# Gathered rows on VectorE in half rows, one behind every 1.6th weight half

## The chip, the cores and the metric

The kernel runs on one core of a Trainium2 chip. The metric is device time in microseconds (us) of one execution. Below, PE is TensorE, DVE is VectorE, ACT is ScalarE, POOL is GpSimd and SP is SyncE, as in the profile; L119 is line 119 of the kernel.

## What is computed

One layer of a decoder trunk over 256 tokens of width 2048 in float32: an RMS norm with two parallel head groups, a cross-attention over 256 memory tokens, and PEER, a retrieval among 16384 experts of one neuron each. The change is in PEER, and only there:

```
q = (xt @ w_pq).reshape(T, PEER_HEADS, 2, PK_DIM // 2)
...
# 8 heads pick 16 experts each for every token: ids, gate
u = u_tab[idb]
act = gelu(einsum('td,thkd->thk', xb, u))
coef = gb * act
out = einsum('thk,thkd->td', coef, v_tab[idb])
...
return rmsnorm(x + out, g_final)
```

## The kernel before

All products run on PE in split precision: a float32 weight is cut into a high part (`whi`, a cast on ACT, L118) and a low part (`wlo`, a subtraction on DVE, L119), and PE multiplies with both. `wsplit` does this for a weight tile of 128 x 2048 in two halves of 1024 columns; three buffers of each kind hold halves (`bufs=3`), and three hold whole weight tiles as they come from memory (`wst`, 1 MB each, loaded by SP's queue, L105).

PEER is computed in two ways at once. For 192 of the tokens all 16384 experts are computed densely: `u_block` (L639 on) takes one tile of 128 experts, makes their activations (32 matmuls, L643 and L644, then an addition on DVE at L647 and Gelu on ACT at L648) and stores them in a ring, and `v_tile` multiplies a tile of `v` with the coefficients of its group (20 matmuls, L873 to L876; behind the last of four tiles DVE adds two results to the residual, L880). The experts come in eight groups e of 16 blocks; a group has 16 v tiles. `coef_half` (L850, and L169 and L170 by `split_plain`) turns the activations of a group into coefficients, with gates that were written to DRAM and are loaded as `gl` by SP's queue. In group e the u tiles of group e+2 are computed beside: two before each half of the coefficients, the other twelve one behind each of the first twelve v tiles, the last four v tiles having none. The groups e=6 and e=7 have no u tiles.

For the other 64 tokens the experts that were picked are gathered: 64 rows of `u_tab` and 64 of `v_tab`, each 128 x 2048 (a row for each partition), by an indirect DMA of POOL (L911) into three buffers (tag `row`). DVE takes a u row with the token's own input and accumulates the products to one number (L924, into `sact`), and adds a v row times its coefficient to `srow` (L927). The generator `gathered` holds this work; it fetches two rows ahead, and each `next` lets one row pass. It is called behind a whole `v_tile`, as often as to have passed 128 rows after 104 v tiles (`slots`, L950), so one or two rows stand behind a v tile. No rows follow the u tiles.

The order of instructions on each engine is made by a scheduler that goes by the order in which they are written and by when it takes their inputs to be ready. `keep_in_program_order` ties an instruction behind the one written just before it for the same engine; what is written later is not tied by it. Each engine runs its own instructions in that order, and one that waits holds up those behind it.

At the end (e=7) `folded` adds `srow` to the last result on PE, `finish` takes squares and the final gains (`gfin`, loaded into a buffer of tag `row`), and the result is normalised and written.

Of the kernel before, what the change touches and what calls it, by code (L numbers as in the profile page):

```python
# [10 lines left out]
F32 = mybir.dt.float32  # L11
# [42 lines left out]
def hybrid_layer(ctx: ExitStack, tc: tile.TileContext, a, out):  # L54
# [40 lines left out]


    n_w = [0]

    def wbuf():
        n_w[0] += 1  # L100
# [10 lines left out]
    def wsplit(st, order=(0, 1)):  # L111

        parts = {}
        for i in order:
            hi = wp.tile([P, 1024], F32R, tag="whi", name=f"whi{n_w[0]}_{i}", bufs=3)
            lo = wp.tile([P, 1024], F32R, tag="wlo", name=f"wlo{n_w[0]}_{i}", bufs=3)
            src = st[:, i * 1024:(i + 1) * 1024]
            S.copy(hi, src)  # L118
            V.tensor_tensor(lo, src, hi.bitcast(F32), op=OP.subtract)  # L119
            parts[i] = hi, lo  # L120

        def part(which):
            return lambda at, n=P: parts[at // 1024][which][:, at % 1024:at % 1024 + n]
        return part(0), part(1)
# [47 lines left out]
    def spread_stats(part, name):  # L172
        ps = sm_tile()
        PE.matmul(ps[:, :T], ones, part, start=True, stop=True)
        r = cst.tile([P, T], F32, name=f"rstd_{name}")
        rstd_of(r, ps[:, :T], D)
        return r

# [450 lines left out]
    with tc.tile_pool(name="ph3", bufs=2) as p3:  # L629
# [2 lines left out]
        srow = p3.tile([P, D], F32, name="srow", bufs=1)  # L632
        sids = p3.tile([P, NP], U32, name="sids", bufs=1)
        sgate = p3.tile([P, NP], F32, name="sgate", bufs=1)
        sact = p3.tile([P, NP], F32, name="sact", bufs=1)
        hpm = lambda k: hp[:, k, :]
        hs = p3.tile([P, KC, 2 * TD], F32R, name="hsc", bufs=1)

# [200 lines left out]
        with tc.tile_pool(name="ph3v", bufs=2) as pv:  # L839
# [65 lines left out]
            def gathered():  # L905

                def fetch(n):
                    if n >= 2 * NP:
                        return None
                    row = pv.tile([P, D], F32, tag="row", name=f"row{n}", bufs=ROWS)  # L910
                    nc.gpsimd.indirect_dma_start(  # L911
                        row, None, a["v_rows" if n >= NP else "u_rows"],
                        bass.IndirectOffsetOnAxis(ap=sids[:, n % NP:n % NP + 1], axis=0))
                    return row

                rows = [fetch(n) for n in range(ROWS - 1)]
                for n in range(2 * NP):
                    rows.append(fetch(n + ROWS - 1))
                    row, j = rows.pop(0), n % NP
                    if n == NP:  # L920
                        S.activation(sact, sact, AF.Gelu)
                        V.tensor_tensor(sact, sact, sgate, op=OP.mult)
                    if n < NP:
                        tc.keep_in_program_order(V.scalar_tensor_tensor(  # L924
                            row, row, 1.0, xrow, op0=OP.mult, op1=OP.mult, accum_out=sact[:, j:j + 1]))
                    else:
                        tc.keep_in_program_order(V.scalar_tensor_tensor(  # L927
                            srow, row, sact[:, j:j + 1], srow, op0=OP.mult, op1=OP.add))
                    yield

            gather = gathered()
            n_gat, n_slot, slots = 0, 0, (NE - 1) * 16 - 8
            gfin = None
            for e in range(NE):
                us = list(range((e + 2) * EB, min((e + 3) * EB, NB)))
# [6 lines left out]
                    if half < 2:  # L942
                        coef_half(e, half)
                for dq, bg in vs:
                    if n_slot == slots + 2:
                        gfin = pv.tile([P, D], F32, tag="row", name="gfin", bufs=ROWS)
                        nc.sync.dma_start(gfin, a["gfin"])
                    v_tile(e, dq, bg, e + 2 >= NE)
                    n_slot += 1
                    while n_gat < min(2 * NP, 2 * NP * n_slot // slots):  # L950
                        next(gather)
                        n_gat += 1
                    if us:
                        u_block(us.pop(0))

# [105 lines left out]
```

## Time and profile before

| | |
|---|---|
| time, median of 3 runs | 2366.49 us (2365.39 to 2367.17) |
| the profiled execution | 2376.57 us |
| its span, first to last instruction | 2374.8 us |
| PE busy | 2209.7 us, 93% of the span |
| DVE busy | 1843.8 us, 78% |
| ACT busy | 1176.4 us, 50% |
| granted TensorE clock, mean | 0.977 |
| DMA, mean over the span | 250 GB/s |

The profile is of one execution. The page gives busy times by engine, the span in slices, and the costliest groups of instructions; further views give busy time by windows, who waited for whom, and the instructions in order of time. Matmuls are pipelined and their ends are modelled, so the busy time of PE is not a measure of its peak. The stage that the change touches begins at about 1195 us.

### The profile page before, as it was taken

What the parts mean: (1) busy time and instruction counts of PE and PEld (TensorE: products, weight loads), DVE (VectorE), ACT (ScalarE), POOL (GpSimd) and SP (SyncE); (2) the same over time, 40 slices, a digit from 0 to 9 for tenths busy, and PEclk for the clock granted to TensorE, in tenths of its full rate; (3) what the DMA queues carried; (4) which work ended last, traced back from release to release, by engine and by line L of the source; (5) the groups of instructions that cost most, each with busy time, mean ns of one, the idle gap of its engine ahead of it and who ended that gap; (6) DMA issues with size and microseconds to landing.
All of it is one profiled execution on the core that took longest, in us unless ns stands there. A gap on an engine that the chain in (4) does not pass through costs nothing.

```text
span 2374.8 us, 31447 instructions
## 1 busy us (share of the span) xinstructions
PE 2209.7 (93%) x12000; PEld 1930.1 (81%) x12000; DVE 1843.8 (78%) x2754; ACT 1176.4 (50%) x1703; POOL 235.3 (10%) x132
## 2 busy tenths in 40 slices
PE   8999999999999988789979999899899899998897
PEld 6888888888888867789968888788788788887675
DVE  7887868744555698999957888878887978888864
ACT  6555547444444543557644444444444445444353
POOL 0000000000000000000001212212221222124100
PEclk9999999999999999999989999999999999999998
DMA  7444445545454533356779899999888998998963
GB/s 268 160 160 160 142 152 203 179 169 179 166 177 165 190 135 132 124 177 249 250 278 350 321 350 349 347 332 375 330 332 320 338 371 338 336 364 331 360 214 124
DMA packets 107928, 593.58 MB, mean 250 GB/s; under 512 B 9600, under 2 KB 35200, under 8 KB 38528
## 3 DMA queue, kind: packets, MB, share of 16 engines
q1 hardware_dynamic: 87472, 444.69, 51.8%
q0 software_dynamic: 18432, 134.23, 15.2%
q10 hardware_dynamic: 1872, 12.65, 1.3%
q8 instruction: 94, 1.54, 0.3%
q14 instruction: 58, 0.48, 0.1%
HBM read 576.84 MB, written 14.68 MB: 249 GB/s over the span
## 4 chain that ended last, share of the span: by engine, by line
PE 64%; issue 15%; DVE 12%; DMA 4%; POOL 3%; ACT 1%; DVEq 0%; POOLq 0%; ACTq 0%
PE mm L133 16%; PE mm L643 9%; PE mm L134 8%; PE mm L644 5%; DVE wlo L119 4%; PE sm L874 4%; PE sm L873 4%; POOL row L911 3%; PE mm L146 2%; PE mm L147 2%; DMA row<-in_v_rows,sids 2%; PE mm L145 2%; PE sm L876 2%; PE sm L808 2%; DVE row L924 1%
## 5 line engine op out<-in xcount | busy, mean ns | idle before, releaser
L119 DVE TENSOR_TENSOR wlo<-wst,whi 128x1024 fp32r<-128x1024 f32 x800 | 969.6, 1222 | 417.0 <-ACT whi L118 409.6
L118 ACT CAST whi<-wst 128x1024 fp32r<-128x1024 f32 x800 | 835.5, 1049 | 866.1 <-PE mm L133 259.5
L643 PE MATMUL mm<-hsc,whi 128*128 128x384 f32 x2048 | 619.8, 370 | 6.9 <-ACT whi L118 6.8
L644 PE MATMUL mm<-hsc,wlo 128*128 128x192 f32 x2048 | 528.6, 259 | 63.3 <-DVE wlo L119 63.3
L644 PEld LDWEIGHTS mm<-hsc,wlo 128*128 128x128 f32 x2048 | 404.3, 197 | 79.0 <-DVE wlo L119 76.1
L643 PEld LDWEIGHTS mm<-hsc,whi 128*128 128x128 f32 x2048 | 397.0, 194 | 12.2 <-ACT whi L118 9.2
L874 PE MATMUL sm<-wlo,coef 128*128 128x512 f32 x896 | 355.8, 397 | 37.3 <-DVE wlo L119 37.3
L873 PE MATMUL sm<-whi,coef 128*128 128x512 f32 x896 | 353.3, 395 | 0.5 <-ACT whi L118 0.5
L911 POOL DMA_INDIRECT row<-in_u_rows,sids x64 | 112.4, 1756 | 1620.1 <-ACT act L648 1196.4
L874 PEld LDWEIGHTS sm<-wlo,coef 128*128 128x128 f32 x896 | 169.9, 190 | 82.3 <-DVE wlo L119 49.0
L873 PEld LDWEIGHTS sm<-whi,coef 128*128 128x128 f32 x896 | 169.4, 189 | 34.8 <-ACT whi L118 0.9
L133 PE MATMUL mm<-h,whi 128*128 128x512 f32 x512 | 184.5, 403 | 0.0
L876 PE MATMUL sm<-whi,coef 128*128 128x512 f32 x448 | 176.8, 395 | 0.0
L911 POOL DMA_INDIRECT row<-in_v_rows,sids x64 | 122.7, 1918 | 373.4 <-DVE srow L927 334.4
L927 DVE SCALAR_TENSOR_TENSOR srow<-row,sact,srow 128x2048 f32<-128x2048 f32 x64 | 150.3, 2348 | 7.1 <-DMA row<-in_v_rows,sids 6.8
L924 DVE SCALAR_TENSOR_TENSOR row<-row,xrow 128x2048 f32<-128x2048 f32 x64 | 145.5, 2286 | 0.2
L134 PE MATMUL mm<-h,wlo 128*128 128x256 f32 x512 | 144.0, 281 | 0.5 <-DVE wlo L119 0.5
L648 ACT ACTIVATE act<-ut 128x192 f32<-128x192 f32 x128 | 47.0, 367 | 151.0 <-DVE ut L647 151.0
L133 PEld LDWEIGHTS mm<-h,whi 128*128 128x128 f32 x512 | 96.3, 188 | 22.2 <-issue 0.3
L133 PE MATMUL mm<-hp,whi 128*128 128x512 f32 x256 | 99.7, 424 | 5.5 <-ACT whi L118 5.5
L876 PEld LDWEIGHTS sm<-whi,coef 128*128 128x128 f32 x448 | 85.1, 190 | 17.2 <-issue 0.2
L134 PEld LDWEIGHTS mm<-h,wlo 128*128 128x128 f32 x512 | 96.7, 189 | 1.4 <-DVE wlo L119 0.9
(337 smaller groups left out, 3263.2 us busy)
## 6 DMA issues: line engine op xcount, KB each, us to landing
wst<-in_uT SPq DMA_DIRECT2D x128, 1024.0 KB, 6.8
wst<-in_v SPq DMA_DIRECT2D x128, 1024.0 KB, 7.2
wst<-in_w_aqk SPq DMA_DIRECT2D x16, 1024.0 KB, 4.9
wst<-in_w_out SPq DMA_DIRECT2D x16, 1024.0 KB, 4.8
wst<-in_w_xk SPq DMA_DIRECT2D x16, 1024.0 KB, 4.9
wst<-in_w_xq SPq DMA_DIRECT2D x16, 1024.0 KB, 4.8
wst<-in_w_xv SPq DMA_DIRECT2D x16, 1024.0 KB, 4.9
wst<-in_w_xo SPq DMA_DIRECT2D x16, 1024.0 KB, 4.8
```

Source lines behind the costliest of these rows:

```text
L118: S.copy(hi, src)
L119: V.tensor_tensor(lo, src, hi.bitcast(F32), op=OP.subtract)
L133: PE.matmul(ps, hi(k * P), mov(k), start=(n == 0), stop=False)
L134: PE.matmul(ps[:, 256:], lo(k * P), mov(k)[:, :256], start=False, stop=(n == len(kcs) - 1))
L643: PE.matmul(ps[:, :2 * TD], hi(k * P), hs[:, k, :2 * TD], start=(k == 0), stop=False)
L644: PE.matmul(ps[:, TD:2 * TD], lo(k * P), hs[:, k, :TD], start=False, stop=(k == KC - 1))
L873: PE.matmul(accs[tt], c_hi, v_hi, start=(c == 0), stop=False)
L874: PE.matmul(accs[tt], c_hi, v_lo, start=False, stop=(tt == 1 and c == EB - 1))
L876: PE.matmul(accs[tt], c_lo, v_hi, start=False, stop=(c == EB - 1))
L911: nc.gpsimd.indirect_dma_start(row, None, a["v_rows" if n >= NP else "u_rows"], bass.IndirectOffsetOnAxis(ap=sids[:, n % NP:n % NP + 1], a ...
L924: tc.keep_in_program_order(V.scalar_tensor_tensor(row, row, 1.0, xrow, op0=OP.mult, op1=OP.mult, accum_out=sact[:, j:j + 1]))
L927: tc.keep_in_program_order(V.scalar_tensor_tensor(srow, row, sact[:, j:j + 1], srow, op0=OP.mult, op1=OP.add))
```

## The change

A row passes DVE in two halves of 1024 columns, each an instruction of its own: the halves of a u row accumulate into two columns (`sact` becomes 128 x 2 x 64), which are added once before Gelu; the halves of a v row add to the halves of `srow`. `next(gather)` lets one half pass. It is no longer called behind v tiles but from `wsplit`, behind each `wlo` of u tiles and v tiles alike, through the hook `beside`: `step` counts weight halves and lets 256 half rows pass over 416 weight halves (96 u tiles and the 112 v tiles of groups e=0 to e=6, two halves each), so one behind every 1.625th. Each half row is tied behind what was written just before it for DVE, now the `wlo`. Rows therefore pass until the end of e=6, and beside the u tiles that stand between two groups as well. The load of `gfin` moves from two v tiles behind the last row to the second v tile of e=7. The normalisation rows of the earlier layers share two buffers (tag `rstd`) in place of one each.

```diff
--- before.py
+++ after.py
@@ -95,6 +95,7 @@
 
 
     n_w = [0]
+    beside = [None]
 
     def wbuf():
         n_w[0] += 1
@@ -118,6 +119,8 @@
             S.copy(hi, src)
             V.tensor_tensor(lo, src, hi.bitcast(F32), op=OP.subtract)
             parts[i] = hi, lo
+            if beside[0]:
+                beside[0]()
 
         def part(which):
             return lambda at, n=P: parts[at // 1024][which][:, at % 1024:at % 1024 + n]
@@ -172,7 +175,7 @@
     def spread_stats(part, name):
         ps = sm_tile()
         PE.matmul(ps[:, :T], ones, part, start=True, stop=True)
-        r = cst.tile([P, T], F32, name=f"rstd_{name}")
+        r = cst.tile([P, T], F32, tag="rstd", name=f"rstd_{name}", bufs=2)
         rstd_of(r, ps[:, :T], D)
         return r
 
@@ -632,7 +635,7 @@
         srow = p3.tile([P, D], F32, name="srow", bufs=1)
         sids = p3.tile([P, NP], U32, name="sids", bufs=1)
         sgate = p3.tile([P, NP], F32, name="sgate", bufs=1)
-        sact = p3.tile([P, NP], F32, name="sact", bufs=1)
+        sact = p3.tile([P, 2, NP], F32, name="sact", bufs=1)
         hpm = lambda k: hp[:, k, :]
         hs = p3.tile([P, KC, 2 * TD], F32R, name="hsc", bufs=1)
 
@@ -914,22 +917,35 @@
                     return row
 
                 rows = [fetch(n) for n in range(ROWS - 1)]
+                half = [slice(0, D // 2), slice(D // 2, D)]
                 for n in range(2 * NP):
                     rows.append(fetch(n + ROWS - 1))
                     row, j = rows.pop(0), n % NP
                     if n == NP:
-                        S.activation(sact, sact, AF.Gelu)
-                        V.tensor_tensor(sact, sact, sgate, op=OP.mult)
-                    if n < NP:
-                        tc.keep_in_program_order(V.scalar_tensor_tensor(
-                            row, row, 1.0, xrow, op0=OP.mult, op1=OP.mult, accum_out=sact[:, j:j + 1]))
-                    else:
-                        tc.keep_in_program_order(V.scalar_tensor_tensor(
-                            srow, row, sact[:, j:j + 1], srow, op0=OP.mult, op1=OP.add))
-                    yield
+                        V.tensor_tensor(sact[:, 0], sact[:, 0], sact[:, 1], op=OP.add)
+                        S.activation(sact[:, 0], sact[:, 0], AF.Gelu)
+                        V.tensor_tensor(sact[:, 0], sact[:, 0], sgate, op=OP.mult)
+                    for i, h in enumerate(half):
+                        if n < NP:
+                            step = V.scalar_tensor_tensor(row[:, h], row[:, h], 1.0, xrow[:, h], op0=OP.mult, op1=OP.mult,
+                                                          accum_out=sact[:, i, j:j + 1])
+                        else:
+                            step = V.scalar_tensor_tensor(srow[:, h], row[:, h], sact[:, 0, j:j + 1], srow[:, h],
+                                                          op0=OP.mult, op1=OP.add)
+                        tc.keep_in_program_order(step)
+                        yield
 
             gather = gathered()
-            n_gat, n_slot, slots = 0, 0, (NE - 1) * 16 - 8
+            n_slot, done = 0, [0, 0]
+            halves = 2 * ((NE - 2) * EB + (NE - 1) * 16)
+
+            def step():
+                done[0] += 1
+                while done[1] < min(4 * NP, 4 * NP * done[0] // halves):
+                    next(gather)
+                    done[1] += 1
+
+            beside[0] = step
             gfin = None
             for e in range(NE):
                 us = list(range((e + 2) * EB, min((e + 3) * EB, NB)))
@@ -942,14 +958,11 @@
                     if half < 2:
                         coef_half(e, half)
                 for dq, bg in vs:
-                    if n_slot == slots + 2:
+                    if n_slot == (NE - 1) * 16 + 1:
                         gfin = pv.tile([P, D], F32, tag="row", name="gfin", bufs=ROWS)
                         nc.sync.dma_start(gfin, a["gfin"])
                     v_tile(e, dq, bg, e + 2 >= NE)
                     n_slot += 1
-                    while n_gat < min(2 * NP, 2 * NP * n_slot // slots):
-                        next(gather)
-                        n_gat += 1
                     if us:
                         u_block(us.pop(0))
```

## Rows read from the trace of the kernel before

**Rows 1.** The page: its first line, part 1 (busy us, share of the span, instructions) for TensorE and VectorE, and the rows of part 2 for TensorE's clock and DMA (40 equal slices of the span; tenths).

```profile
span 2374.8 us, 31447 instructions
...
PE 2209.7 (93%) x12000; PEld 1930.1 (81%) x12000; DVE 1843.8 (78%) x2754; ACT 1176.4 (50%) x1703; POOL 235.3 (10%) x132
...
PEclk9999999999999999999989999999999999999998
DMA  7444445545454533356779899999888998998963
```

**Rows 2.** Windows of the last stage, one for each of the groups e=1 to e=4 and e=6: from:to, length, then busy us (x instructions) of PE, PEld, DVE, ACT and POOL, granted clock, DMA share, GB/s.

```profile
1395.00:1557.00 162.00, 150.14 (x835) 133.09 (x834) 134.93 (x140) 77.38 (x104) 36.61 (x20) 1.00 0.91 343
1557.00:1719.00 162.00, 151.68 (x832) 136.10 (x832) 136.10 (x141) 79.57 (x105) 37.56 (x20) 0.97 0.91 349
1719.00:1885.00 166.00, 154.26 (x838) 137.67 (x836) 134.99 (x126) 78.60 (x105) 34.11 (x19) 0.97 0.89 332
1885.00:2047.00 162.00, 150.55 (x833) 133.87 (x832) 137.10 (x121) 78.47 (x104) 35.54 (x20) 0.99 0.91 349
...
2183.00:2275.00 92.00, 77.71 (x322) 60.59 (x322) 76.52 (x65) 36.76 (x41) 20.66 (x10) 0.98 0.83 318
```

**Rows 3.** Waits of PE from 1246 to 2275 us: who waited, for whom, us in total, times, longest.

```profile
PE mm L644 <- DVE wlo L119: 35.6, 27, 4.2
PE sm L874 <- DVE wlo L119: 34.0, 29, 5.0
PE mm L874 <- DVE wlo L119: 3.3, 5, 0.8
PE mm L643 <- ACT whi L118: 2.6, 4, 1.1
```

**Rows 4.** VectorE's groups of instructions by line from 1195 to 2275 us: line, engine, operation, out<-in, shapes, count | busy us, mean ns of one | idle before them and what ended it.

```profile
L119 DVE TENSOR_TENSOR wlo<-wst,whi 128x1024 fp32r<-128x1024 f32 x414 | 499.0, 1222 | 156.4 <-ACT whi L118 152.2 <-PE mm L644 3.1
L927 DVE SCALAR_TENSOR_TENSOR srow<-row,sact,srow 128x2048 f32<-128x2048 f32 x64 | 150.3, 2348 | 7.1 <-DMA row<-in_v_rows,sids 6.8
L924 DVE SCALAR_TENSOR_TENSOR row<-row,xrow 128x2048 f32<-128x2048 f32 x64 | 145.5, 2286 | 0.2
L880 DVE TENSOR_TENSOR resid<-resid,sm 128x512 f32<-128x512 f32 x52 | 35.5, 684 | 5.3 <-PE sm L876 5.3
...
L170 DVE TENSOR_TENSOR coef<-act,coef 128x512 fp32r<-128x512 f32 (+1 forms) x63 | 32.5, 556 | 0.5 <-PE mm L874 0.5
L850 DVE TENSOR_TENSOR act<-act,gl 128x768 f32<-128x768 f32 x32 | 30.4, 954 | 20.0 <-DMA gl<-gdram 20.0
L924 DVE DVE_READ_ACCUMULATOR row<-row,xrow 128x1 f32 x64 | 5.3, 83 | 0.0
```

**Rows 5.** Timeline of VectorE in group e=1: start us, us, instruction, count.

```profile
1443.56 2.29 DVE L924 SCALAR_TENSOR_TENSOR row<-row,xrow 128x2048 f32<-128x2048 f32 x1
...
1445.77 2.29 DVE L924 SCALAR_TENSOR_TENSOR row<-row,xrow 128x2048 f32<-128x2048 f32 x1
...
1447.98 0.36 DVE L647 TENSOR_TENSOR ut<-mm,ut 128x192 f32<-128x192 f32 x1
1448.25 3.49 DVE L119 TENSOR_TENSOR wlo<-wst,whi 128x1024 fp32r<-128x1024 f32 x3
...
1454.12 2.28 DVE L924 SCALAR_TENSOR_TENSOR row<-row,xrow 128x2048 f32<-128x2048 f32 x1
```

**Rows 6.** Timeline of PE at the same place (in brackets the idle time before, and who ended it).

```profile
1447.78 0.33 PE L643 MATMUL mm<-hsc,whi 128*128 128x384 f32 x1
1449.53 0.36 PE L644 MATMUL mm<-hsc,wlo 128*128 128x192 f32 x1 [1.41 <-DVE wlo L119]
```

**Rows 7.** Windows: 20 us without a wait of PE, and the 10 us with the most DMA traffic of all windows of 10 us from 1250 to 2270 us (columns as in rows 2).

```profile
1450.00:1470.00 20.00, 20.00 (x118) 18.34 (x117) 13.61 (x15) 9.26 (x12) 1.96 (x2) 1.00 0.96 398
...
1940.00:1950.00 10.00, 9.73 (x56) 8.89 (x57) 8.52 (x8) 4.15 (x6) 2.71 (x2) 1.00 1.02 421
```

**Rows 8.** Windows of the stretches at the lower granted clock between 1276 and 2195 us: the first and the last of ten (columns as in rows 2).

```profile
1276.30:1279.70 3.40, 3.40 (x15) 3.40 (x14) 2.71 (x3) 0.00 (x0) 0.38 (x1) 0.50 0.88 323
...
2191.10:2194.50 3.40, 3.30 (x8) 2.63 (x9) 3.40 (x4) 0.00 (x0) 3.10 (x2) 0.50 0.65 205
```

**Rows 9.** Waits of PE for wlo in the first (1358 to 1396 us, two rows) and the last (2164 to 2204 us, one row) of the six windows that hold a group's last four v tiles and the four u tiles, or first v tiles, behind them; the others are 1520:1558, 1682:1720, 1848:1886 and 2010:2048. The fourth row is from 2204:2275, the rest of e=6.

```profile
PE mm L644 <- DVE wlo L119: 2.3, 1, 2.3
PE sm L874 <- DVE wlo L119: 2.1, 1, 2.1
...
PE sm L874 <- DVE wlo L119: 8.3, 4, 5.0
...
PE sm L874 <- DVE wlo L119: 2.7, 3, 1.2
```

**Rows 10.** Window of the second of these (columns as in rows 2).

```profile
1520.00:1558.00 38.00, 33.02 (x186) 28.89 (x186) 30.72 (x36) 18.59 (x28) 8.27 (x4) 1.00 0.96 351
```

**Rows 11.** Waits of VectorE from 1195 to 2275 us.

```profile
DVE wlo L119 <- ACT whi L118: 152.2, 147, 3.2
...
DVE srow L927 <- DMA row<-in_v_rows,sids: 6.8, 4, 2.9
```

**Rows 12.** Timelines of POOL and of VectorE in group e=6: the issue of one gathered row, and its use.

```profile
2187.68 4.27 POOL L911 DMA_INDIRECT row<-in_v_rows,sids  x1 [3.52 <-DVE srow L927]
...
2198.62 2.35 DVE L927 SCALAR_TENSOR_TENSOR srow<-row,sact,srow 128x2048 f32<-128x2048 f32 x1 [2.95 <-DMA row<-in_v_rows,sids]
```

## The prediction

> **What bounds the kernel now.** I began with the page [rows 1]: TensorE (PE) is busy for 93% of the span and VectorE for 78%. The change touches only the last stage, where the 128 gathered rows pass VectorE, so I cut the span into the eight expert groups of that stage. The middle groups take 162 to 166 us each [rows 2]: PE is busy for some 150 to 154 of them and VectorE for 135 to 137, and the 16 DMA engines show a share of 0.89 to 0.91. Nobody is full, yet PE stops; so next I asked what PE waits for. From 1246 to 2275 us it waits 35.6 + 34.0 + 3.3 = 72.9 us, in 61 waits, for the low weight half (wlo) that VectorE makes at L119, and only about 3 us for ScalarE's high half [rows 3]. So PE is the bound, interrupted by a VectorE that is late for moments although it has room on average.
>
> Why it is late can be seen in one place [rows 5, 6]. Two whole rows run at 1443.56 and 1445.77, an addition follows at 1447.98, and only then, at 1448.25, the next wlo, which had been queued behind them. PE starts its matmul on it at 1449.53, after a wait of 1.41 us. The rows held up wlo by 1447.98 - 1443.56 = 4.42 us, 4.69 with the addition, so PE can run on for about 3 us on the halves that lie ready (there are three buffers of each kind). A single row at 1454.12 delays its wlo by 2.2 us, and PE is then busy for 20.00 of the 20 us from 1450 to 1470 [rows 5, 7]. The tolerance is thus between 2.2 and 3.3 us: one row passes, two rows or a row with additions to the residual do not.
>
> [...]
>
> **The change, part by part.** *Row size and pace.* 128 rows become 256 half rows, and L119 hands one over behind each 1.625th weight half (416 halves over 256). A half row has 1024 elements for each partition, as wlo has. Three wlo in a row take 3.49 us [rows 5] with 1.222 for one [rows 4], so one occupies (3.49 - 1.222) / 2 = 1.134 us. A whole u row occupies 2.21 (1445.77 - 1443.56), so 1024 elements more cost 1.076. Two u halves are 2.27, or 0.06 more than the whole. The v row lasts 0.062 longer [rows 4] with its scalar column, so 2.26 to 2.27; two halves of some 1.19 are 0.11 more. The sum is 64 x 0.06 + 64 x 0.11 = 11 us of VectorE. The bounds are 0 (all of it inside VectorE's idle time) and, with no overlap of neighbours, 64 x (2 x 1.222 - 2.286) + 64 x (2 x 1.272 - 2.348) = 23 us. I take 11, since back-to-back neighbours are what the trace shows, and put it beside PE's work: in a middle group it is under 2 us, 135 to 137 becomes 137 to 139, with about 25 idle. If PE's pace rose to 150 us a group, the cover would be 11 us. The accumulator read (83 ns, x64) doubles; the next instruction starts together with it or within the same 0.09 us, so it is worth at most 5 us and I cost it at 0.
>
> [...]
>
> *Order.* Before, a row was traced behind a whole tile, tied behind VectorE's last instruction of it, and one or two came together. Now between two wlo stands at most one half row, 1.13 to 1.19 us, about half of what PE tolerated without a wait. Even behind a pair of additions to the residual (0.6 each) it is 2.4 us, near the lower end of the tolerance. So of the waits outside the turns of the groups I remove nearly all. The turn is the stretch with the last four v tiles of one group and the four u tiles that follow: there VectorE also makes the coefficients (L850, L170; 30.4 + 32.5 us over eight groups [rows 4]). In the six turn windows PE's waits for wlo add up to 28.7 us (first and last of the six are shown) [rows 9]. For e=6 behind its turn it is 2.7 us more [rows 9] and the 3.3 us of L874 into mm [rows 3], 6.0; the rest is 72.9 - 28.7 - 6.0 = 38 us in the even stretches. I take 90% of this, 34 us. Each wait also costs about 0.14 us of refilling (start to start 1.75 where the matmul's own pace is 0.20 [rows 6], less the 1.41): 35 waits, 5 us. Five of the ten clock dips lie outside the turns, 5 x 1.7 = 8.5 us; I take 7.
>
> *Group e=6.* Before, its first eight v tiles carried ten rows in a group of 92 us in which VectorE was 83% busy [rows 2]. Now the ten rows spread over all sixteen tiles. Of the 6.0 us of waits and the refilling I take 7 in all.
>
> *Turns.* The four u tiles of the turn had no rows before; now they get 8 / 1.625 = 4.9 half rows, 5.7 us beside the coefficients' some 7 us, while the last four v tiles go from 4.9 whole rows to 4.9 half rows. VectorE's total in the turn hardly moves (30.7 busy of 38 [rows 10], plus some 2), but the work lies later. Bounds: a gain of 10 (the waits there are partly behind rows, too) or a loss of 34 us, 5.7 x 6, if all of it reaches PE. I take 0, as the total rules: VectorE has 38 - 33 = 5 us left in it.
>
> *Waits that are added or moved.* Behind a half row that waits for its gather stand the wlo halves. The four waits of that kind cost 6.8 us [rows 11], mostly in e=6. With 162 us for the 64 weight halves of a group (2.53 each), rows come 3.25 x 2.53 = 8.2 us apart. A row buffer comes free a half step later than before, since its two halves lie 4.1 us apart; the row fetched into it is needed some 3 x 8.2 - 4.1 - 1.2 = 19 us later, against about 11 from issue to the end of the worst wait (issue 2187.68, use 2198.62) [rows 12]. So nothing. POOL only issues, SP's queue keeps its order but for the load of the final gains, moved from the middle of e=6 into e=7's beginning, three tiles ahead of its reader: nothing, or one weight load's lateness, 3 us. The one addition for the two halves of sact, 0.2 us once, and the shared buffer for the rstd rows, long read when it is written again: nothing. *DMA.* The best 10 us window has 421 GB/s, and PE at full pace already goes with 398 [rows 7]. Group bytes, 345 GB/s x 162 = 56 MB, need 133 us at 421, below PE's 150. I subtract 3 us for late loads.
>
> **The sum**, on the profiled execution (2376.6 us, its span 2374.8): 34 + 5 + 7 + 7 - 3 = 50 us, so 2326.6. This execution lies 10 us above the median of the runs, 0.43%; scaled, 2317.
>
> **Rivals.** *DMA takes over.* For: a share of 0.96 in a turn and in the stall-free 20 us [rows 7, 10]. Against: 133 us against 150. If loads arrive late at 365 GB/s, groups end at 56 / 0.365 = 154 plus the turns' waits, 158: 5 x 4.5 us, 2343. *The waits move into the turns.* Half of the worst case, 17 us, with six more dips of 3.4 us (10) and steady waits only halved: -17 - 10 + 27, about 2366. For: coefficients and rows now meet in the four u tiles. Against: VectorE's total there. *Slower: VectorE's queue stands for the gather.* Since a half row is fixed behind its wlo, an unlanded row blocks the next wlo. If each of the 128 first halves stands 1.7 us, the mean of the four waits seen [rows 11], then VectorE has 1.7 + 1.19 = 2.9 us ahead of the next wlo, against a tolerance from 2.2: 128 x 0.7 = 90 us lost, less the 50, so 2366 + 40 = 2406. It decides from about 1.4 us of standing for each row; against it: rows come every 8 us and are fetched two ahead. *The order does not hold.* The tie is only to the instruction ahead, so halves could still run in pairs: no gain, up to 23 us more on VectorE, of which half may reach PE: 2378.
>
> **How the numbers follow.** Forecast 2317 (0.62), by its own bounds 2290 to 2340; DMA 2343 (0.14); turns 2366 (0.12); gather 2406 (0.07); order 2378 (0.05). The lower end takes in the turns' gain of 10, the other five dips and all of the steady waits. The upper end must reach to the turns case, 2362. Within 0.2% (about what a measurement can tell from no change) is 2361.8 to 2371.2. Faster: 0.62 + 0.14 and a little of the turns case, 0.78; same 0.09; slower 0.13.
>
> **What would show it.** Right: wlo waits of PE outside the turns fall from 38 us to under 8; dips from ten to five or fewer; groups of 150 to 156 us; VectorE's rows x256 with means of some 1.22 to 1.28 us; DMA above 360 GB/s in the middle groups. Wrong: waits of ScalarE for weight loads that grow (DMA), waits at L850 and L170 or behind them in the turns, VectorE idle behind a gather, or two half rows side by side. What would upset the whole is a tolerance smaller than the 2.2 us read from one place.

## The result, and the profile after

The changed kernel takes 2299.31 us (median of 4 runs, 2297.43 to 2301.55) against 2365.94 us (4 runs) for the kernel before: a ratio of 0.9719, 95% interval 0.9703 to 0.9736. The forecast was 2317 us, by its own bounds 2290 to 2340, with an upper end of 2362 for the whole. The profiled execution took 2297.88 us. Lines of the changed kernel lie one to six below those of before: wlo is L120, whi L119, u tiles L646 and L647, v tiles L876, L877 and L879, the half rows L930 and L933.

The page after, its first line and the rows that answer to [rows 1]:

```profile
span 2296.1 us, 31672 instructions
...
PE 2185.4 (95%) x12000; PEld 1915.9 (83%) x12000; DVE 1849.8 (81%) x2947; ACT 1175.2 (51%) x1703; POOL 217.6 (9%) x132
...
PEclk9999999999999999989998999999999999999998
DMA  7444436555544543436779999999999999999963
```

PE is busy for 95% of a shorter span, and the DMA row, which held 8s and 9s in the last stage, is all 9s. The windows of the groups e=1 to e=4 and e=6, with the columns of [rows 2]:

```profile
1374.50:1529.60 155.10, 151.03 (x835) 134.17 (x833) 136.78 (x182) 78.61 (x106) 30.68 (x20) 0.99 0.96 363
1529.60:1678.70 149.10, 147.65 (x835) 133.03 (x834) 135.38 (x179) 78.11 (x105) 32.24 (x20) 1.00 0.97 373
1678.70:1830.80 152.10, 148.51 (x834) 132.79 (x833) 136.92 (x145) 77.58 (x104) 31.67 (x20) 1.00 0.98 367
1830.80:1983.30 152.50, 149.62 (x834) 134.72 (x833) 137.87 (x142) 78.63 (x105) 37.93 (x20) 0.99 0.96 361
...
2115.80:2190.40 74.60, 73.68 (x321) 59.59 (x320) 69.03 (x69) 36.73 (x41) 14.58 (x8) 1.00 0.95 359
```

The middle groups take 149 to 155 us in place of 162 to 166, and e=6, the worst before, 74.6 in place of 92. VectorE does a little more in less time (135 to 138 us of 152), the DMA share went from 0.91 to 0.97, and the granted clock is 0.99 or 1.00 in these groups. PE's waits from 1246 us to 2195 us, a few us into e=7, which answer to [rows 3]:

```profile
PE mm L647 <- DVE wlo L120: 10.0, 18, 1.0
PE sm L877 <- DVE wlo L120: 5.1, 8, 2.1
PE mm L646 <- ACT whi L119: 4.6, 5, 1.1
PE mm L877 <- DVE wlo L120: 0.3, 1, 0.3
```

For wlo these are 10.0 + 5.1 + 0.3 = 15.4 us in 27 waits, from 72.9 in 61; the waits for whi rose from about 3 to 4.6. The waits for wlo can be sorted by what VectorE had worked off without a pause in front of the late wlo, back to the wlo before it (us, and number of waits):

| in front of the late wlo | before | after |
|---|---|---|
| two whole rows, most with other work | 40.9 (20) | none |
| one row (whole before, half after), with or without other work | 29.0 (34) | 7.2 (11) |
| other work alone | 0.4 (2) | 1.2 (2) |
| nothing: VectorE idle, since whi was late | 2.5 (5) | 7.0 (14) |

Late loads, which gathers at an even pace could have helped by themselves, had little part in the waits before: 2.5 us of them at most. VectorE's groups, to be read beside [rows 4]:

```profile
L120 DVE TENSOR_TENSOR wlo<-wst,whi 128x1024 fp32r<-128x1024 f32 x416 | 504.9, 1220 | 98.6 <-ACT whi L119 97.7
L933 DVE SCALAR_TENSOR_TENSOR srow<-row,sact,srow 128x1024 f32<-128x1024 f32 x128 | 163.4, 1277 | 0.0
L930 DVE SCALAR_TENSOR_TENSOR row<-row,xrow 128x1024 f32<-128x1024 f32 x128 | 155.6, 1216 | 4.7 <-DMA row<-in_u_rows,sids 4.7
```

A half u row lasts 1216 ns and a half v row 1277, where the prediction worked with 1.222, the mean of a wlo of that size, and an estimate of 1.272 us. The place that answers to [rows 5]:

```profile
1440.00 1.22 DVE L930 SCALAR_TENSOR_TENSOR row<-row,xrow 128x1024 f32<-128x1024 f32 x1
...
1441.14 1.22 DVE L120 TENSOR_TENSOR wlo<-wst,whi 128x1024 fp32r<-128x1024 f32 x1
...
1455.51 1.22 DVE L930 SCALAR_TENSOR_TENSOR row<-row,xrow 128x1024 f32<-128x1024 f32 x1
...
1456.65 1.22 DVE L120 TENSOR_TENSOR wlo<-wst,whi 128x1024 fp32r<-128x1024 f32 x1
1457.79 1.22 DVE L930 SCALAR_TENSOR_TENSOR row<-row,xrow 128x1024 f32<-128x1024 f32 x1
...
1459.80 2.46 DVE L120 TENSOR_TENSOR wlo<-wst,whi 128x1024 fp32r<-128x1024 f32 x2
```

Between two wlo stands one half row, never two here: at 1455.51 a half row, at 1456.65 its wlo, at 1457.79 the next half row. What waits in front of the wlo at 1456.65 began 1.14 us earlier; in [rows 5] it was 4.69.

### The profile page after: what moved, and what is told of

Read it like the earlier page. It is cut to its first block, busy times and chain, and to the rows that moved or that the text cites. A ratio compares the mean times of both kernels' runs of the same rounds, so it can differ in the third digit from the quotient of the medians.

```text
span 2296.1 us, 31672 instructions
## 1 busy us (share of the span) xinstructions
PE 2185.4 (95%) x12000; PEld 1915.9 (83%) x12000; DVE 1849.8 (81%) x2947; ACT 1175.2 (51%) x1703; POOL 217.6 (9%) x132
## 4 chain that ended last, share of the span: by engine, by line
PE 77%; DVE 12%; DMA 7%; issue 2%; ACT 2%; DVEq 0%; ACTq 0%
PE mm L136 16%; PE mm L646 13%; PE mm L137 9%; PE mm L647 6%; PE sm L877 6%; PE sm L876 6%; DVE wlo L120 5%; DMA wst<-in_uT 4%; PE sm L879 3%; PE mm L149 2%; PE mm L150 2%; PE mm L148 2%; PE sm L811 2%; DMA wst<-in_v 2%; ACT whi L119 1%
## 5 line engine op out<-in xcount | busy, mean ns | idle before, releaser
L119 ACT CAST whi<-wst 128x1024 fp32r<-128x1024 f32 x800 | 835.2, 1050 | 824.2 <-PE mm L136 258.7
L120 DVE TENSOR_TENSOR wlo<-wst,whi 128x1024 fp32r<-128x1024 f32 x800 | 972.6, 1221 | 350.2 <-ACT whi L119 346.1
L646 PE MATMUL mm<-hsc,whi 128*128 128x384 f32 x2048 | 608.8, 365 | 8.9 <-ACT whi L119 8.9
L647 PE MATMUL mm<-hsc,wlo 128*128 128x192 f32 x2048 | 523.8, 256 | 42.5 <-DVE wlo L120 42.0
L647 PEld LDWEIGHTS mm<-hsc,wlo 128*128 128x128 f32 x2048 | 398.0, 194 | 56.5 <-DVE wlo L120 53.6
L646 PEld LDWEIGHTS mm<-hsc,whi 128*128 128x128 f32 x2048 | 391.9, 191 | 14.2 <-ACT whi L119 11.2
L877 PE MATMUL sm<-wlo,coef 128*128 128x512 f32 x896 | 352.3, 393 | 5.4 <-DVE wlo L120 5.1
L876 PE MATMUL sm<-whi,coef 128*128 128x512 f32 x896 | 352.3, 394 | 0.0
L914 POOL DMA_INDIRECT row<-in_u_rows,sids x64 | 97.7, 1527 | 1577.0 <-ACT act L651 1189.0
L877 PEld LDWEIGHTS sm<-wlo,coef 128*128 128x128 f32 x896 | 168.9, 188 | 46.0 <-DVE wlo L120 12.7
L876 PEld LDWEIGHTS sm<-whi,coef 128*128 128x128 f32 x896 | 168.6, 188 | 34.0 <-issue 0.2
L879 PE MATMUL sm<-whi,coef 128*128 128x512 f32 x448 | 175.9, 393 | 0.0
L933 DVE SCALAR_TENSOR_TENSOR srow<-row,sact,srow 128x1024 f32<-128x1024 f32 x128 | 163.4, 1277 | 0.0
L930 DVE SCALAR_TENSOR_TENSOR row<-row,xrow 128x1024 f32<-128x1024 f32 x128 | 155.6, 1216 | 4.7 <-DMA row<-in_u_rows,sids 4.7
L879 PEld LDWEIGHTS sm<-whi,coef 128*128 128x128 f32 x448 | 84.3, 188 | 17.3 <-issue 0.2
```

The source lines that it names most:

```text
L646: PE.matmul(ps[:, :2 * TD], hi(k * P), hs[:, k, :2 * TD], start=(k == 0), stop=False)
L647: PE.matmul(ps[:, TD:2 * TD], lo(k * P), hs[:, k, :TD], start=False, stop=(k == KC - 1))
L876: PE.matmul(accs[tt], c_hi, v_hi, start=(c == 0), stop=False)
L877: PE.matmul(accs[tt], c_hi, v_lo, start=False, stop=(tt == 1 and c == EB - 1))
L879: PE.matmul(accs[tt], c_lo, v_hi, start=False, stop=(c == EB - 1))
L914: nc.gpsimd.indirect_dma_start(row, None, a["v_rows" if n >= NP else "u_rows"], bass.IndirectOffsetOnAxis(ap=sids[:, n % NP:n % NP + 1], a ...
```

## The experiments

Twelve kernels were measured in three groups, each with the kernel before beside it. Times are medians; ratios are to the kernel before of the same group, whose own median was 2368 to 2371 us. The waits are those of PE for wlo from 1246 us to a few us into e=7, as in [rows 3].

| kernel | us | ratio, 95% interval | waits for wlo, us | e=6, us |
|---|---|---|---|---|
| before, a second trace | 2371.2 (one run) | | 67.4 | 88.8 |
| halves behind v tiles | 2385.8 | 1.0066 (1.0049 to 1.0083) | 78.4 | 96.0 |
| old order to the end of e=6 | 2359.9 | 0.9955 (0.9938 to 0.9972) | 57.9 | 97.4 |
| whole rows, even, behind tiles | 2337.5 | 0.9849 (0.9812 to 0.9887) | 42.2 | 76.7 |
| whole rows, even, behind wlo | 2319.8 | 0.9793 (0.9771 to 0.9815) | 31.3 | 77.1 |
| half rows beside v tiles alone | 2312.0 | 0.9764 (0.9744 to 0.9785) | 27.0 | 96.6 |
| half rows, none in the turns | 2308.9 | 0.9749 (0.9722 to 0.9777) | 19.5 | 76.4 |
| quarter rows | 2303.8 | 0.9725 (0.9695 to 0.9755) | 22.6 | 76.9 |
| changed kernel again | 2294.1 | 0.9673 (0.9642 to 0.9703) | 16.6 | 77.1 |
| rows of one column | 2281.6 | 0.9636 (0.9599 to 0.9673) | 7.4 | 73.3 |
| no gathers | 2264.5 | 0.9563 (0.9523 to 0.9604) | 6.4 | 73.9 |
| without the tie | 2478.6 | 1.0459 (1.0426 to 1.0492) | 142.9 | 72.5 |

The group times are read from the first matmul of a group's v tiles to that of the next. The changed kernel has 0.9719 in the first measurement and 0.9673 in a later group, so comparisons between groups are worth no more than half a per cent.

**Size or pace.** My theory was that a wlo should never have two rows in front of it, whatever makes that so; the rival, that the size of one piece is what counts. Two kernels take the parts of the change alone. The first passes whole rows from the hook:

```diff
-                half = [slice(0, D // 2), slice(D // 2, D)]
+                half = [slice(0, D)]
...
-                        V.tensor_tensor(sact[:, 0], sact[:, 0], sact[:, 1], op=OP.add)
...
-                while done[1] < min(4 * NP, 4 * NP * done[0] // halves):
+                while done[1] < min(2 * NP, 2 * NP * done[0] // halves):
```

> Whole rows instead of half rows, one behind every 3.25th weight half, from the same hook as in the changed kernel. Pace theory (what helped is that rows come singly and evenly, beside u tiles as well; one whole row of 2.21 to 2.26 us still lies under what TensorE tolerates): 2300 to 2318 us, waits of TensorE for wlo from 1246 us to the end of e=6 under 30 us. Size theory (what helped is that no instruction of over 2 us stands ahead of a wlo): 2330 to 2360 us, with over 50 us of these waits.

It took 2319.8 us with 31.3 us of waits, both just outside what the pace theory expected (2318 and 30): 63 to 74% of the gain in ratio (0.0207 of 0.0327 or of 0.0281, the changed kernel's two ratios) without a half row.

```profile
PE mm L647 <- DVE wlo L120: 19.0, 24, 2.3
PE sm L877 <- DVE wlo L120: 11.7, 15, 1.7
```

The longest wait is 2.3 us, where the changed kernel has 1.0 before the last turn; a whole row alone does not always pass. The kernel before shows it as well, against the tolerance that the prediction read from one place: in e=6 a single row stands between two wlo (2216.77 and 2220.16), and PE waits 0.84 us.

```profile
2217.90 2.35 DVE L927 SCALAR_TENSOR_TENSOR srow<-row,sact,srow 128x2048 f32<-128x2048 f32 x1
2220.16 1.22 DVE L119 TENSOR_TENSOR wlo<-wst,whi 128x1024 fp32r<-128x1024 f32 x1
...
2221.44 0.50 PE L874 MATMUL mm<-wlo,coef 128*128 128x512 f32 x1 [0.84 <-DVE wlo L119]
```

The second kernel keeps halves but puts them where the whole rows were (the hook is not set, and the loop behind `v_tile` stands as before, with two calls for a row):

```diff
-            beside[0] = step
...
                     n_slot += 1
+                    while n_gat < min(2 * NP, 2 * NP * n_slot // slots):
+                        next(gather)
+                        next(gather)
+                        n_gat += 1
```

> Half rows, but two or four of them in a row behind a v tile as before the change, at the old pace and up to the old end. Pace theory: as before the change or a little slower, 2362 to 2380 us, since the same 2.2 to 4.7 us stand ahead of a wlo and VectorE works 11 us more. Size theory: the scheduler can put a wlo between two halves, so at least half of the gain is there, 2300 to 2335 us.

It took 2385.8 us, longer than before. The timeline of VectorE in this kernel shows why:

```profile
1441.92 1.22 DVE L930 SCALAR_TENSOR_TENSOR row<-row,xrow 128x1024 f32<-128x1024 f32 x1
...
1443.07 1.22 DVE L930 SCALAR_TENSOR_TENSOR row<-row,xrow 128x1024 f32<-128x1024 f32 x1
...
1444.21 1.22 DVE L930 SCALAR_TENSOR_TENSOR row<-row,xrow 128x1024 f32<-128x1024 f32 x1
...
1445.36 0.35 DVE L650 TENSOR_TENSOR ut<-mm,ut 128x192 f32<-128x192 f32 x1
1445.63 1.21 DVE L930 SCALAR_TENSOR_TENSOR row<-row,xrow 128x1024 f32<-128x1024 f32 x1
...
1446.77 3.49 DVE L120 TENSOR_TENSOR wlo<-wst,whi 128x1024 fp32r<-128x1024 f32 x3
```

Four half rows run from 1441.92 to 1446.77 with only the addition of a u tile among them, and the next wlo stands behind all of them, 4.85 us late, where [rows 5] had 4.69. The scheduler put no wlo between these halves. So the pieces are worth nothing by themselves here (78.4 us of waits for wlo, against 72.9 and 67.4 before): the size theory falls, as the main cause.

**Spread or place.** The next step takes the kernel before and changes one number, so that its rows pass until the end of e=6.

```diff
-            n_gat, n_slot, slots = 0, 0, (NE - 1) * 16 - 8
+            n_gat, n_slot, slots = 0, 0, (NE - 1) * 16
...
-                    if n_slot == slots + 2:
+                    if n_slot == slots + 1:
```

> The kernel before with one number changed: 128 whole rows over 112 v tiles in place of 104, so that they pass until the end of e=6. If the gain in e=6 (92 to 75 us) comes from the spread alone: e=6 at 82 us or less, 2350 to 2358 us. If it needs the half rows or the place behind a wlo: e=6 at 86 us or more and 2360 to 2368 us.

The second branch came out in e=6, with 97.4 us, and missed in time by 0.1 us (2359.9), but for neither of its reasons. Counted in v tiles, e=6 gets 16 of 112 parts, 18 rows in place of ten, so what was spread thinner elsewhere (the middle groups fell to 157 to 160 us) was piled up here:

```profile
2156.30:2253.70 97.40, 80.96 (x322) 60.88 (x321) 87.13 (x68) 36.84 (x41) 35.20 (x18) 0.96 0.95 362
```

VectorE is busy for 87 of 97 us. So this kernel does not test what it was made for. The change counts weight halves, and e=6 holds 32 of 416: its rows stay at ten and go over sixteen v tiles in place of eight. That this spread is what shortens e=6 shows in the two kernels with whole rows at the even pace, 76.7 and 77.1 us. The same piling up shows in half rows that are handed over beside v tiles alone:

```diff
-            halves = 2 * ((NE - 2) * EB + (NE - 1) * 16)
+            halves = 2 * (NE - 1) * 16
...
-            beside[0] = step
...
+                    beside[0] = step
                     v_tile(e, dq, bg, e + 2 >= NE)
+                    beside[0] = None
```

> Half rows behind weight halves, but of v tiles alone: 256 over 224 halves, so one, at times two, behind each half of a v tile, and none beside the u tiles, the four of a turn among them. Pace theory: the v tile takes about 2.3 + 2.7 us of VectorE in 4.6 us of TensorE, evened out by the u tile behind it, so most of the gain stays but not in the last four v tiles: 2310 to 2335 us. If the four u tiles of the turn are better without rows, as a rival holds: under 2297 us.

It took 2312.0 us, within the range of the pace theory, but the reason given was off: the middle groups take 148 to 154 us as in the changed kernel, last four v tiles included, and the loss is e=6 with 96.6.

To part the place behind a wlo from the pace, whole rows were passed at the even pace behind whole tiles of either kind:

```diff
-            beside[0] = step
...
                             u_block(b)
+                            step()
...
                     n_slot += 1
+                    step()
                     if us:
                         u_block(us.pop(0))
+                        step()
```

with `halves` counting tiles, and rows whole.

> Whole rows at the even pace, one behind every 1.625th tile of either kind, u or v, but behind the whole tile, as before the change, and not inside the weight split. If the pace is the cause (single rows, beside u tiles too, ten of them in e=6): as the whole rows from the hook, ratio to before 0.975 to 0.984. If the place right behind a wlo is the cause: ratio 0.990 or more.

The ratio is 0.9849, a little above what the pace alone should give and with an interval that reaches the expected range. PE's waits:

```profile
PE mm L647 <- DVE wlo L120: 32.0, 32, 5.3
PE sm L877 <- DVE wlo L120: 8.8, 13, 1.4
```

It lies between the two branches, so neither theory is enough alone. The pace, with the ten rows of e=6 spread, brings about half of the gain. The place behind a wlo (42.2 to 31.3 us of waits) and the halving (31.3 to 15.4) bring the rest: by the ratios about 13 us, give or take 10, and 17 to 28 us.

**The tie.** One line taken out of the changed kernel:

```diff
-                        tc.keep_in_program_order(step)
```

> The changed kernel without the tie of a half row behind the wlo written just before it (one line less). If the hook's place decides and the tie does little, since the scheduler goes by the order of writing: within 0.3% of the changed kernel. If the tie is what keeps rows from standing in front of a wlo: rows move ahead to where their gather is taken to have landed, VectorE waits for gathers, 2310 us or more.

2478.6 us, 8% more than the 2294.1 with it. My own theory had allowed at most 0.3%. The two windows are the groups e=0 and e=3:

```profile
1217.60:1447.90 230.30, 170.70 (x835) 146.80 (x833) 202.07 (x292) 75.47 (x102) 67.97 (x47) 0.91 0.97 373
1874.40:2020.30 145.90, 145.90 (x834) 132.85 (x833) 94.83 (x101) 78.19 (x104) 0.00 (x0) 1.00 0.71 242
```

The rows moved ahead: all have passed by 1821 us, so e=0 takes 230 us and e=3, without a row, 145.9. And they wait for their gathers. VectorE's waits from 1190 to 2370 us, with one such place (the issue on POOL, then the row on VectorE):

```profile
DVE srow L933 <- DMA row<-in_v_rows,sids: 34.5, 22, 4.0
DVE row L930 <- DMA row<-in_u_rows,sids: 33.9, 26, 3.9
```

```profile
1585.57 1.68 POOL L914 DMA_INDIRECT row<-in_v_rows,sids  x1 [3.41 <-DVE srow L933]
...
1596.72 2.48 DVE L933 SCALAR_TENSOR_TENSOR srow<-row,sact,srow 128x1024 f32<-128x1024 f32 x2 [3.23 <-DMA row<-in_v_rows,sids]
...
1599.39 1.21 DVE L120 TENSOR_TENSOR wlo<-wst,whi 128x1024 fp32r<-128x1024 f32 x1
```

The row issued at 1585.57 is used at 1596.72 after 3.23 us of standing, and the wlo behind it starts at 1599.39. This is the mechanism of the rival that I called slower, a queue of VectorE that stands for the gather: 68 us of it here, against 4.7 in the changed kernel. It is not all of the 184 us that the kernel is slower. TensorE waits 126 us more for wlo, and of its 142.9 us, sorted as above, 67 stand behind two or three half rows: the rows are crowded into the first groups, and VectorE works 202 of the 230 us of e=0. So halves side by side, the rival named for an order that does not hold, are there too, and what each costs alone is not shown. With the tie a row is held back, and only the first gather is waited for (4.67 us).

**Turns, and smaller pieces.** Half rows everywhere but beside the four u tiles ahead of a group's v tiles:

```diff
-            halves = 2 * ((NE - 2) * EB + (NE - 1) * 16)
+            halves = 2 * ((NE - 2) * (EB - sum(U_BEFORE)) + (NE - 1) * 16)
...
-            beside[0] = step
...
+                beside[0] = step
                 for dq, bg in vs:
...
                         u_block(us.pop(0))
+                beside[0] = None
```

> The changed kernel, half rows behind each 1.44th weight half, but none beside the four u tiles ahead of a group's v tiles, where the coefficients are made. If rows and coefficients collide there, as the turns rival holds: the middle groups 1 to 3 us shorter each, 2286 to 2296 us. If VectorE's total in the turn is all that counts: 2297 to 2306 us, as the changed kernel or a little slower through denser rows elsewhere.

2308.9 us, above both ranges, and the groups 152.6 to 154.4: no better. Rows in the turn cost less than the denser rows elsewhere that replace them; that they cost nothing there is not shown. Quarter rows (`half` with four slices, `sact` with four columns a row, 512 steps over the 416 halves):

> Quarter rows of 512 columns, at the same pace (512 over 416 weight halves, so one or two behind each). One occupies about 0.6 us, 128 rows cost VectorE some 16 to 30 us more than half rows. Pace theory (anything under the tolerance of 2.2 us is alike): 2297 to 2310 us, through the dearer pieces. Size theory (the smaller the better): 2280 to 2295 us.

2303.8 us, as the pace theory expects: smaller pieces than a half row brought no more (22.6 us of waits for wlo, against 15.4 and 16.6 with halves). A quarter lasts 685 and 746 ns, so four of a u row are busy for 2.74 us where a whole took 2.29.

**What is left.** Two kernels leave work out to see what the rows still cost in the changed one. First VectorE's part:

```diff
-                half = [slice(0, D // 2), slice(D // 2, D)]
+                half = [slice(0, 1), slice(D // 2, D // 2 + 1)]
```

> The changed kernel with the work of a half row cut to one of its 1024 columns (left out: the other columns, so its result is not the layer's); every gather stays. VectorE loses some 280 us of work in the last stage. If VectorE's room is what still costs something: TensorE's waits for wlo after 1246 us fall from 16 us to under 5, 2275 to 2288 us. If late loads are the rest, as the DMA rival holds: waits that begin with a late wst stay and it is 2289 to 2300 us.

Then the transfers:

```diff
+                    if n >= ROWS:
+                        return kept[n % ROWS]
...
+                    kept.append(row)
...
-                            step = V.scalar_tensor_tensor(row[:, h], row[:, h], 1.0, xrow[:, h], op0=OP.mult, op1=OP.mult,
+                            step = V.scalar_tensor_tensor(row[:, h], xrow[:, h], 1.0, xrow[:, h], op0=OP.mult, op1=OP.mult,
```

> The changed kernel with three gathers in place of 128 (left out: the rows behind the third, VectorE reads the same three buffers again and, for u rows, the token's own input twice; so its result is not the layer's); VectorE's work stays. DMA loses 134 MB of 594. If late loads are the rest: the share of DMA falls from 0.97 to about 0.65, ScalarE's waits for wst go, the middle groups take 146 to 149 us, 2270 to 2288 us. If VectorE's room is the rest: 2289 to 2300 us, groups of 150 us and more.

The same group, e=2, in the first and in the second:

```profile
1532.30:1680.00 147.70, 146.47 (x833) 132.93 (x832) 96.70 (x177) 78.28 (x104) 22.83 (x20) 1.00 0.99 377
```

```profile
1519.10:1666.00 146.90, 146.21 (x835) 132.92 (x834) 135.80 (x180) 78.15 (x105) 0.00 (x0) 1.00 0.71 242
```

Without VectorE's work the group takes 147.7 us, at a DMA share of 0.99; without the gathers 146.9, at 0.71, though VectorE works 135.8 us of it. So both are part of what is left. The times are 2282 and 2264, by the ratios 9 to 20 and 26 to 37 us under the changed kernel; the waits for wlo of the first, 7.4 us, and the time of the second lie outside what was expected (under 5; 2270 or more). The four groups e=1 to e=4 take 594.6 and 590.9 us where the changed kernel takes 608.9, so there the two are nearly alike, 14 and 18 us; most of what still parts them lies in e=0 (161.5 and 150.8 us; 158.8 in the changed kernel), and is not explained. ScalarE's waits for weight loads are 59.2 + 50.2 us in the changed kernel from 1246 us on, 36.9 + 34.0 in the kernel before, and none among the longer ones without gathers. But they are 93.3 + 52.2 with rows of one column, which is faster, and where TensorE waits 7.4 us for wlo and 2.7 for whi: most of this standing does not reach TensorE. Of TensorE's own waits, 6.1 us begin with a late load in the changed kernel (8.2 in its second trace).

**The two kernels again.** The kernel before left a second trace, and the changed one ran beside it.

> The kernel before, for a second trace: the first was of an execution 10 us above the median. If those 10 us were chance: the stretch up to 1195 us is up to 8 us shorter, the last stage has the same groups within 3 us each and 65 to 80 us of waits for wlo behind 1246 us.

> The changed kernel once more, beside the next two: ratio to before 0.970 to 0.974. If it differs from the first by more than 0.2%, comparisons across chips are worth no more than that.

The second trace of before has a span of 2369.4 us, 5.4 less than the first, with 1.5 of it ahead of the last stage; its middle groups agree within 2 us, the last that has u tiles only within 5.4 and e=6 within 3.1, a little more than the 3 expected. The changed kernel's ratio of 0.9673 is lower than expected, and outside the first interval.

## Why the prediction was right, and where its sum was not

The mechanism holds. wlo was late behind whole rows, for 69.9 of 72.9 us of waits, and singly and evenly passed half rows leave 7.2; the direction and the range were right. The gain of 67 us was larger than the 50 of the sum, by the terms below. One reading was wrong: "one row passes". Single rows stood in front of 29.0 us of the waits before, 11.4 of it with nothing else beside them, so there is no fixed tolerance of 2.2 to 3.3 us. The forecast suffered little from it, since half rows are shorter still.

*Waits in the even stretches*: 38 us before, of which I took 34. After, 15.4 - 7.7 (turns) - 0.3 (e=6) - 2.1 (the turn into e=7) leaves 5.3, a gain of 33. Right.

*Group e=6*: I took 7. Its 6.0 us of waits behind the turn fell to 0.3. The group as a whole went from 92 to 74.6 us (88.8 to 77.1 in the second traces), since most of the sixth turn's 8.3 us lies in it as well.

*Turns*: I took 0, "as the total rules". This is the term that was mis-sized. The waits in the six windows fell from 28.7 to 2.2 + 1.8 + 0.7 + 1.6 + 0.9 + 0.5 = 7.7 us, by 21 where my own bound for the gain was 10. The first and the last of the six after, which answer to [rows 9]:

```profile
PE mm L647 <- DVE wlo L120: 2.2, 4, 0.8
...
PE sm L877 <- DVE wlo L120: 0.5, 1, 0.5
```

The window of the second, which answers to [rows 10], has VectorE busy for 34.03 of 38 us in place of 30.72, and yet its PE waits are 1.8 us in place of 4.4:

```profile
1492.00:1530.00 38.00, 35.34 (x192) 31.44 (x191) 34.03 (x49) 20.22 (x31) 5.56 (x5) 0.96 0.94 352
```

A total of 33 of 38 had been forecast; it was not the total that made PE wait there but, as everywhere, the whole rows: 26.8 of the 28.7 us stood behind one or two of them. That the four u tiles now carry rows beside the coefficients costs nothing that the kernel without them could show. So neither of my two arguments about the turns (a loss from the four u tiles, none from the last v tiles) was right.

*Clock*: I took 7 us, from five dips at 1.7. No run shows the 1.7: in the dip at 1515.2 of the changed kernel the pairs of L646 and L647 start 0.53 us apart, and right behind it 0.28, so 3.4 us of it cost 1.6. Ten stretches at a granted clock of 0.50, 37 us long, became three of 3.4 us (the first and the last are shown, to be read beside [rows 8]; the last lies in e=7): (37.3 - 10.2) / 2 = 14 us is an estimate from the granted clock of 0.50; at 1.6 us of 3.4 it is 13. Four of the five dips of the turns went with the waits of the turns. The first two of the three left, at 1515.2 and 1894.1, stand behind a late weight load: ScalarE had waited 5.10 and 5.59 us for it, and PE then waited for whi and wlo, 0.90 + 0.82 and 0.86 + 0.81 us.

```profile
1515.20:1518.60 3.40, 3.40 (x15) 3.40 (x14) 3.40 (x6) 1.27 (x2) 0.00 (x0) 0.50 0.86 301
...
2194.50:2197.90 3.40, 3.40 (x10) 2.63 (x9) 2.40 (x3) 1.04 (x1) 0.00 (x0) 0.51 0.70 205
```

*VectorE's extra work*: 11 us forecast. What follows a half u row starts 1.14 to 1.15 us behind its start (1440.00 to 1441.14 above), so two are 2.29 against 2.21: 5 us for the 64 u rows. Three v halves in a row, which the kernel without the tie has, last 3.67 us with 1.28 for one, so 1.195 apart, 0.12 more a row: 8 us. That makes 13, beside PE's work but for what lies in the 7.2 us of waits behind half rows. That the extra work needs a cover shows in the halves behind v tiles, at 15 us more than the kernel before beside them.

*DMA*: I took 3 us, and gave its rival, 2343 us, a chance of 0.14. The sign named for it came, for ScalarE's waits for weight loads grew from 70.9 to 109.4 us, but little of it reached PE: the waits of PE that begin with a late load went from 1.2 to 6.1 us in the first traces and from 8.1 to 8.2 in the second. DMA did not take over; without the gathers the kernel would be 26 to 37 us faster.

*The slower rival*, a queue that waits for the gather, is real, but only without the tie. That kernel was 109 us above the kernel before beside it (2478.6 - 2478.6 / 1.0459), where I had worked out 40, but with rows crowded together as well, so the price of the standing alone is not shown.

The terms nearly close. The second pair of traces differs by 68.1 us from PE's 6600th matmul (1252.5 us before, 1247.3 after) to its 11660th, about where e=7 begins. In this stretch the waits give 67.4 - 16.6 = 51 us, the clock, by the same estimate, (37.4 - 6.8) / 2 = 15 and 27 waits fewer, at the 0.14 us that the prediction read at one place, another 4, 70 in all. The first pair has 76.6 us there, and the terms give 80. Outside the stretch the second pair gains 5.2 us ahead of it and loses 4.6 in e=7; that the spans, 2369.4 - 2300.7 = 68.7 us apart, are so near to the sum is luck. Of the 5.2 us, 3.8 are there at PE's 6400th matmul, where the stage begins (1194.6 and 1190.8 us), and 7.5 in the first pair (1196.1 and 1188.6). In the other kernels that matmul starts at 1186.8 to 1195.9 us, so this is not put down to the change.

One cost was not forecast. The first half row now comes before the first coefficients of e=0 and stands 4.67 us for its gather on VectorE, and PE waits 9.74 us behind it and a load of the gates (1206.75 us). In the kernel before, PE waited there as well, for the gates (5.90 us at 1215.9 and more): 14.0 us for wlo before and 14.6 after from 1190 to 1246 us, so next to nothing was lost in waits. A start of the rows behind these coefficients, which the kernel without rows in the turns has, left 13.1 us there.

Open are two things. First, e=7, which holds no rows, takes 105.7 us after the change in place of 100.1. A wait of 2.1 us at its start and two dips more than before (at 2194.5 and 2214.9; that at 2259.3 has its like before, at 2337.9) make, at 1.6 a dip, 2.1 + 2 x 1.6 = 5.3 of it. It comes with VectorE's rows up to the end of e=6: e=7 takes 100.1 us where the rows end earlier (halves behind v tiles) or are cut to one column, which has the gains' load at its new place, too, 101.7 without the tie, and 102.9 or more in every kernel whose rows run to the end of e=6 in full, 103.7 without the gathers. Why the clock falls at 2214.9, behind a wait of 2.47 us that stood there before without a dip, is not shown. Second, whether an earlier load of the weights would give back the rest: it needs another buffer of 1 MB, and was not tried.

## What to carry to other kernels

An engine with idle time can still stop another by what stands in front of one instruction in its queue (VectorE, busy for 78% of the span, made TensorE wait 72.9 us for wlo): look at how late the needed result may come, in many places and not in one (here a whole row of 2.2 us passed at one place and made TensorE wait 0.84 us at another), and pass side work in small pieces, one behind each needed result. Cutting the pieces without moving them gained nothing (2386 us), moving them without cutting gained two thirds to three quarters, and the tie that keeps them where they were put was worth more than either (2479 us without it). Count the pace in what the side work competes with, weight halves here and not tiles of one kind, or it piles up where that kind stands alone.

## What the runs showed of the hardware

The 16 DMA engines ran at a share of 0.97 over 800 us (1300 to 2100 of the changed kernel) and 366 GB/s while PE was busy for 782 of the 800, and a share of 0.99 still went with a group of 147.7 us, within 2 us of the 145.9 that a group without any rows took: in these stretches a share near one was not by itself a bound. Against that stands the kernel without gathers, whose VectorE works as much (135.8 us of e=2, where the changed kernel has 135.4), and which is 26 to 37 us faster by the ratios.
